# Hybrid attention and DeltaNet decoder trunk on one core: q of the second half in ring tiles, its z projection gated behind the first half's LayerNorm, and a weaker gate for the seven-product MLP

## The chip, the cores and the metric

The kernel runs on one core of one Trainium2 chip. The metric is device time in microseconds (us), the median of the runs of one program. The program before was run three times.

## What is computed

Input x is 1024 tokens by 1024 features in float32; two layers follow each other. Layer 0 is a hybrid mixer, layer 1 a recurrent block, and each is followed by a LayerNorm over `alpha*x + mixer(x)`, a squared-ReLU MLP with 4096 hidden features, and a second LayerNorm over `alpha*x + mlp(x)`.

```python
proj = x @ w_in                                  # layer 0
qa, ka, va, qkv_b, z, beta_logit, a_logit = split_cols(proj, HYB_SPLITS)
o_a = sliding_window_attention(rope(qa), rope(ka), va, sinks)   # 8 query heads, 2 kv heads, window 128
qb, kb, vb = split(silu(causal_dwconv(qkv_b, conv_w)))          # 4 heads of 128
o_b = gated_delta_rule(l2norm(qb), l2norm(kb), vb, g, beta)
o_b = rmsnorm(o_b) * norm_w * silu(z)
mix = concat([o_a, o_b]) @ w_out
...
x = layer_norm(alpha * x + mix)
x = layer_norm(alpha * x + square(relu(x @ w1)) @ w2)
```

## The kernel before

**Halves and streams.** The 1024 tokens are worked as two halves of 512, c = 0 and c = 1. Each half is one Python generator, `stream(c)` (line 1373): hybrid mixer, `mix_out` (output projection and LayerNorm), MLP and LayerNorm of layer 0, then the same for layer 1. Beside the two streams run small generators called mixers: the DeltaNet heads (`head_mid`, line 967), attention (`attn_prep`, `attn_block`), the LayerNorms, and so on. They are spawned by the streams.

**Arithmetic.** Every large product is made of three matmuls on operands that are split into a rounded high part and a rest (`mm3`). A weight block of 128 x 1024 is loaded by SP's DMA queue into a tile `ws` (3 buffers), ScalarE or, for every fifth block, VectorE makes the high part `wh`, VectorE makes the rest `wl` (`wblock`, line 349; 3 buffers each). A projection of 128 features by 512 tokens (`proj_fm`) is 24 matmuls of 512 columns on one weight block. The heads and the attention use plain float32 matmuls and transposes of 32 to 128 columns; in what follows they are the small matmuls. They write to the four `mx` banks, the projections to the four `mm` banks.

**The order on TensorE is a planner's.** `class Clock` (line 60) keeps estimated end times of all operations. The loop at line 1402 takes, at each step, a mixer whose next inputs are ready by that estimate, or else one more product of a stream: of the two streams the one in the earlier phase first, and if that is blocked, the other. TensorE's instructions get a fixed order in this way; VectorE, ScalarE and SP are then put in order by a timeline scheduler. Each engine works its own list strictly in that order on the chip.

**Buffers as gates.** A generator goes on when its buffers are free: `need("g", n)` for n of 14 granules (`g`, 128 x 2048, line 25), and the rings of 128 x 512 tiles `t` (11), `s` (10) and `f` (4, line 29). For c = 0, heads use rings `t` and `s` in turn, for c = 1 only `t`, so of c = 1 one head is in work at a time.

**The order in the hybrid mixer of c = 1** (`hybrid`, line 1269; the branch `if c` follows `zs`). The projections k, q, v of head 0 come first (`head_front`), then k and v of attention (`kv_proj`), then q of attention (`q_proj`, line 760, which puts its four blocks into one granule, `st["qg"]`), then k, q, v of head 1. The projections that cannot be used yet are parked (`park`, line 913): made on TensorE, copied to a tile `r` and stored in DRAM as `parked_b`; six for heads 2 and 3, and four z, one for each head. They are loaded back into `f` tiles when a head wants them: by `head_front` with x = None, and, for the four z, by `zs` (line 1298), which waits until c = 0 has the key `"ln0"`, set in `mix_out` (line 1334) when the granules of the LayerNorm's output are claimed. `head_z` (line 949) works silu(z) out of a loaded block in two ScalarE and two VectorE steps. The rope of `attn_prep` (line 796) reads the q blocks; the granule is given back at the end of `attn_preps` (line 1244).

**The MLP** (`mlp`, line 529) works the 4096 hidden features in four quarters of two parts. `straight(e)` does one part with plain products: four projections of 24 matmuls and 96 matmuls with the second weight. From some even part on, `first(j)` makes the eight hidden projections of a quarter j ahead and `seven(j)` multiplies that quarter in seven instead of eight block products, 168 instead of 192 matmuls, at the price of summed weights made by DMA and of two granules. The loop before stays with `straight` while this does not hold: c = 1 itself, or c = 1 has begun its output projection in this layer, and two granules are free, and the part is even (line 718).

Of the kernel before, what the change touches and what calls it, by code (L numbers as in the profile page):

```python
# [20 lines left out]
CH = 512  # L21
NT = CH // P
KT = D // P
ALPHA = 4 ** 0.25
GB = 14
# [188 lines left out]
def trunk(ctx: ExitStack, tc, I, out):  # L214
# [21 lines left out]
    rings = dict(RINGS, g=GB)  # L236
# [12 lines left out]
    def gran(dt=F32):  # L249
        return take("g", gpool.tile([P, 2048], dt, tag="g", name=nm("g")))  # L250
# [4 lines left out]
    def ts(r, dt=F32):  # L255
        return tl(r, dt)[:, :512]

    def free(r, *tiles):
        rings[r] += len(tiles)
        spare[r] += [t.name for t in tiles]  # L260
        assert rings[r] <= (GB if r == "g" else RINGS[r])

    def need(r, n=1):
        return wait(lambda: rings[r] >= n)
# [4 lines left out]
    def wait(cond):  # L269
        while not cond():  # L270
            yield BLOCK
# [7 lines left out]
    def v4(a):  # L279
        return a.rearrange("p (a b) -> p a b", a=4)  # L280
# [248 lines left out]
    def mlp(layer, c, yT, yg, ls, res, tail=False):  # L529
# [185 lines left out]

        hids = {}
        e = 0
        while e < 8 and not ((c == 1 or sts[1].get("op", -1) >= layer) and rings["g"] >= 2 and e % 2 == 0):
            if e == 7:
                res["start"]()  # L720
            yield from straight(e, e == 7)
            e += 1
# [36 lines left out]

    def q_proj(c, x, st, oT):  # L760
        ps = yield from proj_tm([I["hin_q"][i] for i in range(4)], x, 512)
        st["qg"] = gran()
        for n in range(NT):
            oT.quad(0, n)
            S.copy(st["qg"][:, n * CH:(n + 1) * CH], ps[n])
        yield UNIT

    def kv_proj(c, x, st, oT, pre):
# [25 lines left out]
        V.tensor_tensor(x4[:, :, :, 1, :], a4[:, :, :, 1, :], b4[:, :, :, 0, :], ALU.add)  # L794

    def attn_prep(c, n, st, tl, o):
        q, kr = v4(st["qg"][:, n * CH:(n + 1) * CH]), st["k"][n]
        yield from need("f", 2)
        a, b, qs = tl[n % 2], ts("f"), v4(ts("f"))
        rope(kr.unsqueeze(1), kr.unsqueeze(1), 1, n, a[:, :128], b[:, :128])  # L800
        rope(qs, q, 4, n, a, b)
        yield at(kr, qs)
        ps = mx_ps()
        PE.transpose(ps[:, :P], kr, ident)
        kT = cpool.tile([P, P], F32, tag="kT", name=nm("kT"), bufs=4)
        V.tensor_copy(kT, ps[:, :P])
        ps = mx_ps()
        for g in range(4):
            PE.transpose(ps[:, g * P:(g + 1) * P], qs[:, g, :], ident)
        free("f", b, qs)  # L810
        S.copy(a, ps)
        o["qT"], o["kT"] = a, kT
        yield at(a, kT)
        o["ok"] = True
# [429 lines left out]
    def attn_preps(c, st, o):  # L1244
        yield from wait(lambda: c == 0 or sts[0].get("att") == 4)
        angles["t"] = clk.tile("angles", 1, cpool.tile([P, 256], F32, tag="angles", name=nm("angles")))
        DA.dma_start(angles["t"], I["angles"][c])
        for n in range(NT):
            yield from wait(lambda: st.get("att", 0) >= n - 1)
            yield from attn_prep(c, n, st, slot["tl"], o[n])  # L1250
        free("g", st["qg"])

    def attention(c, st, oT, o):
        for n in range(NT):
# [14 lines left out]
    def hybrid(c, x, oT, st, rs):  # L1269
        d = [dict() for _ in range(4)]  # L1270
        if c == 0:
            slot["tl"] = slots(8)
            yield from kv_proj(c, x, st, oT, lambda k2: load_xT(c, x, k2))
            DS.dma_start(csb, I["consts"])
        else:
            yield from wait(lambda: "x" in st)
            yield from head_front(c, 0, x, d[0], rs[0])
            yield from wait(lambda: sts[0].get("att", 0) >= 2)
            yield from kv_proj(c, x, st, oT, None)
        spawn(delta_scalars(c, st))  # L1280

        def q():
            yield from need("g", 3)
            yield from q_proj(c, x, st, oT)
            o = [dict() for _ in range(NT)]
            spawn(attention(c, st, oT, o))
            spawn(attn_preps(c, st, o))
        def begin(h):
            yield from wait(lambda: h - st.get("scan", 0) < len(rs))
            spawn(head_mid(c, h, st, d[h], oT, rs[h % len(rs)]))  # L1290

        def later(h):
            yield from begin(h)
            for i in range(h + 1, 4):
                yield from head_front(c, i, None, d[i], rs[0])
                yield from begin(i)

        def zs():
            yield from wait(lambda: "ln0" in sts[0])
            yield from need("g", 2)  # L1300
            oT.quad(1, 0)
            for h in range(4):
                yield from head_z(h, None, oT, d[h])

        def mixer(g):
            spawn((r if r is not UNIT else lambda: 0.0) for r in g)

        if c:
            yield from q()
            yield from begin(0)  # L1310
            yield from head_front(c, 1, x, d[1], rs[0])
            mixer(later(1))
            mixer(zs())
            for h in (2, 3):
                for j in range(3):
                    yield from park(h * 4 + j, x)
            for h in range(4):
                yield from park(h * 4 + 3, x)
        for h in range(0 if c else 4):
            yield from head_front(c, h, x, d[h], rs[h % len(rs)])  # L1320
            yield from begin(h)
            if h == 1:
                yield from q()
                yield from need("g", 2)
                yield from head_z(0, x, oT, d[0])
                yield from head_z(1, x, oT, d[1])
                spawn(load_x(1, xTs[1]))
        if c == 0:
            yield from head_z(2, x, oT, d[2])
            yield from head_z(3, x, oT, d[3])  # L1330
        x.free()
        yield from wait(lambda: st.get("mids") == 4 and st.get("att") == 4)

    def mix_out(w, oT, resid, which, r, s, t, hold):
        yield from after(t)
        yield from need("g", 2)
        s["yg"] = [gran() for _ in range(2)]
        ls = ln_stats()
        s["yT"] = ActT()
        f = dict(n=0, start=lambda: spawn(layernorm(s["yg"], ls, which, r, s["yT"], f)))  # L1340
        yield from out_proj(w, oT, resid, s["yg"], ls, f)
        s["ln0"]["op"] = which // 2
        yield from wait(hold)
        yield from need("g", 4)
        s["yT"].claim()
        s["ln0"]["ln0"] = True
        yield from wait(lambda: "done" in f)

    def mlp_ln(layer, c, s, r, last):
        ls = ln_stats()  # L1350
# [22 lines left out]
    def stream(c):  # L1373
        s = dict(ln0=st[c])
        xT, oT = xTs[c], ActT()
        yield from hybrid(c, xT, oT, st[c], ("t", "s") if c == 0 else ("t",))
        yield from mix_out(I["hout"], oT, lambda n: I["x"][c * CH + n * P:c * CH + (n + 1) * P, :], 0,
                           "s" if c == 0 else "t", s, st[c]["t"], lambda: c == 0 or "m7" in sts[0])
        phase[c] = 1
# [168 lines left out]
```

## Time and profile before

| what | value |
|---|---|
| median of 3 runs | 2271.6 us (2271.26 to 2272.66) |
| profiled execution, its own time | 2273.03 us |
| its span on the core | 2271.3 us |
| matmul busy / weight load busy | 97% / 79% of the span |
| VectorE (DVE) / ScalarE (ACT) busy | 68% / 46% |
| mean granted TensorE clock | 0.994 |

The profile is taken in one execution, whose own time is 1.7 us above its span and 1.4 us above the median of the runs. Matmuls overlap and their ends are modelled, so 97% busy is no measure of how dense they are. Engines are PE (matmuls), PEld (weight loads of TensorE), DVE, ACT, POOL and SP. All operations of the rows carry line 178, 206 or 210, the helpers that record them, so they are told apart by their tiles.

### The profile page before, as it was taken

The page shows a single profiled execution, that of the slowest core. Times are in us where ns is not written, and L with a number is a line of the kernel's source. Part 1 is how long each engine was busy: PE and PEld are TensorE (multiplying, and loading weights), DVE is VectorE, ACT ScalarE, POOL GpSimd, SP SyncE. Part 2 cuts the span into 40 slices and gives each one's busy share as a digit, 9 for nine tenths or more (in the row PEclk, how much of TensorE's full clock was granted, in tenths as well). Part 3 has the DMA queues.
Part 4 walks back from the last instruction along what each step waited for, and adds up shares of the span by engine and source line. Part 5 has one row for each costly group of instructions (what it writes and reads, how often), then busy time and mean ns, then how long its engine had stood idle before and what let it go on. Part 6 is the DMA issues. An engine that isn't in the chain of part 4 may idle for free.

```text
span 2271.3 us, 31951 instructions
## 1 busy us (share of the span) xinstructions
PE 2210.8 (97%) x12436; PEld 1787.7 (79%) x12436; DVE 1546.5 (68%) x2809; ACT 1049.1 (46%) x1878; POOL 28.9 (1%) x56
## 2 busy tenths in 40 slices
PE   8999999979999999999999999999999999999997
PEld 7767877757878887888888878778788887888886
DVE  7787776576555567586567898685565657776477
ACT  5465456244422344454444677373434444444442
POOL 0000000000000000000000000000000000000000
PEclk9999999999999999999999999999999999999999
DMA  4121223256677666677775333323523443444341
GB/s 168 59 78 39 94 77 115 81 171 185 192 200 225 207 215 199 208 255 222 232 216 184 130 130 129 122 75 102 181 98 127 140 144 128 150 169 145 122 165 66
DMA packets 89944, 337.46 MB, mean 149 GB/s; under 512 B 9920, under 2 KB 10304, under 8 KB 81600
## 3 DMA queue, kind: packets, MB, share of 16 engines
q1 hardware_dynamic: 76688, 280.56, 35.7%
q0 software_dynamic: 4608, 33.56, 7.8%
q10 hardware_dynamic: 8496, 21.30, 2.7%
q8 instruction: 97, 1.59, 0.3%
q14 instruction: 55, 0.45, 0.1%
HBM read 324.37 MB, written 78.12 MB: 177 GB/s over the span
## 4 chain that ended last, share of the span: by engine, by line
PE 86%; DVE 8%; ACT 4%; DMA 1%; issue 1%; SPq 0%; ACTq 0%; DVEq 0%
PE mm L206 67%; PE mx L206 17%; DVE g L178 2%; PE mx L210 2%; DVE wl L178 1%; DVE s L178 1%; ACT g L178 1%; DVE t L178 1%; DVE f L178 1%; ACT s L178 1%; ACT wh L178 1%; DMA parked<-r 1%; ACT t L178 1%; ACT f L178 0%; DMA f<-parked 0%
## 5 line engine op out<-in xcount | busy, mean ns | idle before, releaser
L206 PE MATMUL mm<-g,wh 128*128 128x512 f32 x2816 | 883.7, 395 | 2.4 <-ACT g L178 1.2
L178 DVE TENSOR_TENSOR wl<-ws,wh 128x1024 fp32r<-128x1024 f32 (+1 forms) x444 | 538.9, 1214 | 395.7 <-ACT wh L178 391.0
L178 ACT CAST wh<-ws 128x1024 fp32r<-128x1024 f32 (+1 forms) x356 | 371.4, 1043 | 685.2 <-PE mm L206 587.0
L206 PEld LDWEIGHTS mm<-g,wh 128*128 128x128 f32 x2816 | 520.3, 188 | 110.0 <-DVE g L178 3.1
L206 PE MATMUL mm<-g,wl 128*128 128x512 f32 x1408 | 549.6, 390 | 0.0
L206 PE MATMUL mm<-wh,s 128*128 128x512 f32 x1152 | 376.9, 394 | 0.7 <-DVE g L178 0.7
L206 PEld LDWEIGHTS mm<-g,wl 128*128 128x128 f32 x1408 | 264.6, 188 | 55.8
L206 PEld LDWEIGHTS mm<-wh,s 128*128 128x128 f32 x1152 | 217.0, 188 | 46.5 <-ACT s L178 1.1
L206 PE MATMUL mm<-wh,g 128*128 128x512 f32 (+1 forms) x768 | 239.7, 383 | 6.4 <-ACT wh L178 6.2
L206 PE MATMUL mm<-wl,s 128*128 128x512 f32 x576 | 225.1, 391 | 0.0
L206 PE MATMUL mx<-wh,s 128*128 128x512 f32 x576 | 188.0, 392 | 1.2 <-DVE s L178 1.2
L206 PEld LDWEIGHTS mm<-wh,g 128*128 128x128 f32 x768 | 142.9, 191 | 33.4 <-ACT wh L178 6.2
L178 ACT CAST s<-g 128x512 fp32r<-128x512 f32 x172 | 104.7, 622 | 105.5 <-PE mm L206 53.5
L178 DVE TENSOR_TENSOR s<-g,s 128x512 fp32r<-128x512 f32 x172 | 116.4, 688 | 45.0 <-ACT s L178 44.9
L206 PE MATMUL mm<-wl,g 128*128 128x512 f32 (+1 forms) x384 | 144.1, 375 | 0.4 <-DVE wl L178 0.4
L206 PEld LDWEIGHTS mx<-wh,s 128*128 128x128 f32 x576 | 108.2, 188 | 24.0 <-DVE s L178 2.0
L206 PEld LDWEIGHTS mm<-wl,s 128*128 128x128 f32 x576 | 108.6, 189 | 21.4 <-issue 0.2
L206 PE MATMUL mx<-wl,s 128*128 128x512 f32 x288 | 112.2, 390 | 0.0
L178 DVE CAST wh<-ws 128x1024 fp32r<-128x1024 f32 x88 | 60.5, 688 | 69.2 <-PE mm L206 62.4
L178 DVE TENSOR_TENSOR g<-g,mm 128x512 f32<-128x512 f32 x136 | 89.4, 684 | 13.4 <-PE mm L206 12.8
L178 ACT ACTIVATE g<-mm 128x512 f32<-128x512 f32 x100 | 59.1, 591 | 77.0 <-PE mm L206 77.0
L206 PEld LDWEIGHTS mm<-wl,g 128*128 128x128 f32 x384 | 73.3, 191 | 11.8 <-DVE wl L178 0.7
(234 smaller groups left out, 2397.3 us busy)
## 6 DMA issues: line engine op xcount, KB each, us to landing
ws<-w SPq DMA_DIRECT2D x232, 512.0 KB, 3.3
ws<-t SPq DMA_DIRECT2D x96, 512.0 KB, 3.4
t<-w POOLq DMA_DIRECT2D x32, 1024.0 KB, 9.0
ws<-hin_fm SPq DMA_DIRECT2D x32, 512.0 KB, 3.3
t<-w SPq DMA_DIRECT2D x16, 1024.0 KB, 7.1
t<-t SPq DMA_DIRECT2D x16, 1024.0 KB, 7.3
ws<-rin SPq DMA_DIRECT2D x32, 512.0 KB, 3.3
ws<-hout SPq DMA_DIRECT2D x16, 512.0 KB, 3.5
```

Source lines behind the costliest of these rows:

```text
L178: r = f(*a, **k)
L206: ins = self.pe.matmul(out, lhsT, rhs, start=start, stop=stop, skip_group_check=fresh)
L210: return self._pe(self.pe.transpose(out, x, ident), out, [x], 0.00042 * 2 * out.shape[-1])
```

## The change

Four things are done. In the half c = 1, `q_proj` writes its four blocks to four tiles of ring `s` (each given back once its rope is done) instead of a granule, and waits for two granules and four `s` tiles instead of three granules; while the `s` tiles are not free, up to six of the parked projections of heads 2 and 3 are made ahead of it. The output projection of c = 0 waits until the projections of head 1 of c = 1 are done (`"front"`). The z of c = 1 wait for the end of the LayerNorm of c = 0 (`"lnd"`) instead of its start (`"ln0"`). And the seven-product form of the MLP may begin, in layer 0, also when three of the four heads of c = 1 are through their scan and four granules are free.

```diff
@@ mlp
-        while e < 8 and not ((c == 1 or sts[1].get("op", -1) >= layer) and rings["g"] >= 2 and e % 2 == 0):
+        room = lambda: rings["g"] >= (2 if c == 1 or sts[1].get("op", -1) >= layer else
+                                      4 if layer == 0 and sts[1].get("scan", 0) >= 3 else GB)
+        while e < 8 and not (room() and e % 2 == 0):
@@ q_proj
-        st["qg"] = gran()
+        if c == 0:
+            g = st["qg"] = gran()
+            st["q"] = [g[:, n * CH:(n + 1) * CH] for n in range(NT)]
+        else:
+            st["q"] = [ts("s") for _ in range(NT)]
         for n in range(NT):
             oT.quad(0, n)
-            S.copy(st["qg"][:, n * CH:(n + 1) * CH], ps[n])
+            S.copy(st["q"][n], ps[n])
@@ attn_prep
-        q, kr = v4(st["qg"][:, n * CH:(n + 1) * CH]), st["k"][n]
+        q, kr = v4(st["q"][n]), st["k"][n]
...
         rope(qs, q, 4, n, a, b)
+        if c:
+            free("s", st["q"][n])
@@ attn_preps
-        free("g", st["qg"])
+        if c == 0:
+            free("g", st["qg"])
@@ hybrid
-            yield from need("g", 3)
+            yield from need("g", 3 - c)
+            yield from need("s", 4 * c)
...
         def zs():
-            yield from wait(lambda: "ln0" in sts[0])
+            yield from wait(lambda: "lnd" in sts[0])
...
         if c:
+            ahead = [h * 4 + j for h in (2, 3) for j in range(3)] + [h * 4 + 3 for h in range(4)]
+            while rings["s"] < 4 and len(ahead) > 4:
+                yield from park(ahead.pop(0), x)
             yield from q()
             yield from begin(0)
             yield from head_front(c, 1, x, d[1], rs[0])
+            st["front"] = True
             mixer(later(1))
             mixer(zs())
-            for h in (2, 3):
-                for j in range(3):
-                    yield from park(h * 4 + j, x)
-            for h in range(4):
-                yield from park(h * 4 + 3, x)
+            for b in ahead:
+                yield from park(b, x)
@@ mix_out
         yield from wait(lambda: "done" in f)
+        s["ln0"]["lnd"] = True
@@ stream
+        if c == 0:
+            yield from wait(lambda: "front" in st[1])
```

No engine has more or fewer instructions than before: 10842 matmuls in the program's list of both, of the same shapes, and 2809 on DVE. Four copies and the sixteen rope products that read them have an `s` tile where they had a granule. Up to the end of `kv_proj` of c = 1, TensorE's list is the same. In the output projection of c = 0 lies the main difference: before, `q_proj`, three projections and six parked ones stand between `kv_proj` and it; now two parked ones, `q_proj`, three projections and one parked one. Behind it stand four parked ones before and seven now.

**SP's list, from the end of q_proj to the first block of the output projection.** `ws` is a weight block, `hin_q` the weight of q, `hin_fm` of the other projections, `hout` of the output projection, `r` the tile that is parked. Before:

```order
L178 DMA ws_447_3315<-hin_q 128x1024
L178 DMA ws_457_3364<-hin_fm 128x1024
L178 DMA ws_490_3539<-hin_fm 128x1024
L178 DMA ws_501_3653<-hin_fm 128x1024
L178 DMA ws_505_3692<-hin_fm 128x1024
L178 DMA ws_512_3764<-hin_fm 128x1024
L178 DMA ws_527_3913<-hin_fm 128x1024
L178 DMA ws_545_4044<-hin_fm 128x1024
L178 DMA ws_553_4093<-hin_fm 128x1024
L178 DMA ws_565_4162<-hin_fm 128x1024
L178 DMA parked_8_3760<-r_511_3761 128x512
L178 DMA ws_591_4301<-hout 128x1024
```

Now, from the second of the two parked ones that stand ahead of q_proj:

```order
L178 DMA ws_435_3215<-hin_fm 128x1024
L178 DMA ws_447_3286<-hin_q 128x1024
L178 DMA ws_451_3325<-hin_q 128x1024
L178 DMA ws_455_3364<-hin_q 128x1024
L178 DMA ws_458_3394<-hin_q 128x1024
L178 DMA parked_8_3211<-r_434_3212 128x512
L178 DMA ws_470_3437<-hin_fm 128x1024
L178 DMA parked_9_3278<-r_442_3279 128x512
L178 DMA ws_505_3647<-hin_fm 128x1024
L178 DMA ws_514_3726<-hin_fm 128x1024
L178 DMA ws_518_3765<-hin_fm 128x1024
L178 DMA ws_531_3829<-hout 128x1024
```

Nine projections stood between q and the output projection, four stand there now.

**DVE's list at the end of the LayerNorm of c = 0.** Splits of its transposed output are the rows `g<-mx` (before g_660 and g_662, now g_632 and g_634); `f` tiles and the rows that read them are z; `wl` with `ws_738` before, and with `ws_698`, `ws_722`, `ws_731` now, is a weight block of the MLP. Before:

```order
L178 TENSOR_TENSOR g_662_4821<-mx_699_5050,g_661_4820 128x4x128
L178 TENSOR_TENSOR g_660_4819<-mx_700_5063,g_659_4818 128x4x128
L178 TENSOR_TENSOR t_612_4413<-mx_701_5082,csb_75 128x128
L178 TENSOR_TENSOR g_668_4833<-f_683_4941,g_667_4832 128x512
L178 TENSOR_TENSOR g_662_4821<-mx_702_5100,g_661_4820 128x4x128
L178 TENSOR_TENSOR wl_740_5390<-ws_738_5387,wh_739_5389 128x1024
L178 TENSOR_TENSOR t_612_4413<-t_612_4413,mx_706_5142 128x128
L178 SCALAR_TENSOR_TENSOR f_693_5030<-f_693_5030,f_694_5031 128x512
L178 STREAM_TRANSPOSE t_612_4413<-t_612_4413 128x128
L178 TENSOR_TENSOR g_668_4833<-f_693_5030,g_667_4832 128x512
L178 TENSOR_TENSOR t_612_4413<-mx_707_5161,csb_75 128x128
L178 TENSOR_TENSOR g_660_4819<-mx_708_5179,g_659_4818 128x4x128
```

Now:

```order
L178 TENSOR_TENSOR g_634_4604<-mx_670_4884,g_633_4603 128x4x128
L178 TENSOR_TENSOR g_632_4602<-mx_671_4894,g_631_4601 128x4x128
L178 TENSOR_TENSOR wl_685_4984<-ws_683_4981,wh_684_4983 128x1024
L178 TENSOR_TENSOR wl_700_5035<-ws_698_5032,wh_699_5034 128x1024
L178 SCALAR_TENSOR_TENSOR f_704_5044<-f_704_5044,f_705_5045 128x512
L178 TENSOR_TENSOR wl_724_5157<-ws_722_5154,wh_723_5156 128x1024
L178 SCALAR_TENSOR_TENSOR f_706_5051<-f_706_5051,f_707_5052 128x512
L178 TENSOR_TENSOR g_703_5043<-f_704_5044,g_702_5042 128x512
L178 TENSOR_TENSOR g_703_5043<-f_706_5051,g_702_5042 128x512
L178 TENSOR_TENSOR t_479_3461<-g_702_5042,g_703_5043 128x512
L178 TENSOR_TENSOR wl_733_5248<-ws_731_5245,wh_732_5247 128x1024
L178 TENSOR_TENSOR g_634_4604<-mx_688_5016,g_633_4603 128x4x128
```

The rows before hold the second to the fifth of the eight splits, with two of the four z among them and the others behind; now no z stands ahead of the seventh split (`mx_671`), and two stand between it and the eighth (`mx_688`).

**SP's list at the start of the output projection of c = 1.** `w1_0` and `w2_0` are the MLP's weights. Before:

```order
L178 DMA ws_997_7180<-w2_0 128x1024
L178 DMA ws_1005_7228<-w2_0 128x1024
L178 DMA ws_1008_7258<-w2_0 128x1024
L178 DMA t2_0_2_115<-t1_0_2_113 128x2048
L178 DMA ws_1018_7304<-hout 128x1024
```

Now:

```order
L178 DMA ws_1010_7254<-w2_0 128x1024
L178 DMA ws_1015_7290<-w1_0 128x1024
L178 DMA t4_0_2_116<-t2_0_2_115 128x2048
L178 DMA ws_1020_7333<-w1_0 128x1024
L178 DMA ws_1031_7377<-hout 128x1024
```

Two of the eight hidden projections of the first seven-product quarter have moved ahead of the output projection of c = 1. The quarter itself is the same one, the third: four parts are straight before it in both.

## Rows read from the trace of the kernel before

**Rows 1.** The page: its span and busy times.

```profile
span 2271.3 us, 31951 instructions
PE 2210.8 (97%) x12436; PEld 1787.7 (79%) x12436; DVE 1546.5 (68%) x2809; ACT 1049.1 (46%) x1878; POOL 28.9 (1%) x56
```

**Rows 2.** Stages by their windows: length, busy us of PE, PEld, DVE, ACT and POOL with the number of instructions, granted clock, DMA share, GB/s. The stages are the projections and parked ones ahead of the output projection of c = 0, the stretch behind it up to the MLP's first matmul, and the four straight parts.

```profile
290.00:380.10 90.10, 87.40 (x745) 62.97 (x744) 62.21 (x172) 44.91 (x123) 0.00 (x0) 1.00 0.30 100
...
443.00:486.70 43.70, 34.61 (x377) 27.80 (x375) 38.01 (x96) 20.57 (x35) 0.00 (x0) 0.88 0.47 164
486.70:711.20 224.50, 220.56 (x1660) 175.87 (x1661) 131.37 (x294) 82.67 (x184) 10.17 (x14) 1.00 0.69 195
```

**Rows 3.** The same columns, in slices of 10 us around the MLP's first matmul, and in a stretch of the seven-product MLP.

```profile
470.00:480.00 10.00, 3.49 (x94) 2.43 (x95) 8.74 (x15) 4.05 (x7) 0.00 (x0) 0.78 0.98 375
480.00:490.00 10.00, 8.49 (x152) 6.30 (x143) 7.16 (x14) 4.84 (x11) 0.00 (x0) 0.71 0.54 166
490.00:500.00 10.00, 7.17 (x58) 5.32 (x56) 8.12 (x15) 3.29 (x7) 1.03 (x2) 1.00 0.29 74
...
1000.00:1250.00 250.00, 249.37 (x1114) 205.66 (x1113) 168.23 (x203) 112.33 (x156) 6.78 (x10) 1.00 0.70 215
```

**Rows 4.** Whom PE waited for from 443 to 500 us: total us, times, longest us.

```profile
PE mx L206 <- DVE t L178: 9.3, 4, 3.9
PE mx L206 <- DVE lnw L178: 1.4, 1, 1.4
PE mm L206 <- ACT g L178: 1.2, 1, 1.2
PE mm L206 <- DVE g L178: 0.3, 1, 0.3
```

**Rows 5.** PE in order of time: start us, us, engine, line, operation, out<-in, shape, count, and in brackets the idle time before it with what ended it. The first two rows are the first matmuls of two parked projections, 24 matmuls apart; 486.73 is the MLP's first matmul; 699.28 is the last row of small matmuls in the four straight parts.

```profile
443.00 0.62 PE L206 MATMUL mm<-g,wh 128*128 128x512 f32 x2
...
448.44 0.62 PE L206 MATMUL mm<-g,wh 128*128 128x512 f32 x2
...
471.01 0.45 PE L206 MATMUL mx<-t 32*32 32x32 f32 x32
471.39 0.66 PE L210 MATMUL mx<-csb,g 128*128 128x128 f32 x4
471.80 0.71 PE L206 MATMUL mm<-g,wh 128*128 128x512 f32 x2
472.35 0.40 PE L206 MATMUL mm<-g,wl 128*128 128x512 f32 x1
475.36 0.51 PE L206 MATMUL mx<-t 32*32 32x32 f32 x32 [2.61 <-DVE t L178]
479.76 0.65 PE L206 MATMUL mx<-t 32*32 32x32 f32 x32 [3.90 <-DVE t L178]
480.34 1.11 PE L210 MATMUL mx<-csb,g 128*128 128x128 f32 x4
...
486.73 0.50 PE L206 MATMUL mm<-g,wh 128*128 128x512 f32 x1 [1.17 <-ACT g L178]
...
699.28 0.60 PE L210 MATMUL mx<-csb,t 128*128 128x128 f32 x4
```

**Rows 6.** DVE in order of time, the same columns. 446.21 is the last statistics operation of the output projection of c = 0, 488.29 the last split of its LayerNorm.

```profile
446.21 0.64 DVE L178 BATCH_NORM_STATS2 lns<-g 128x6 f32<-128x512 f32 x1
...
452.15 0.15 DVE L178 TENSOR_TENSOR lnw<-lnw 128x2 f32<-128x2 f32 x1
452.22 0.15 DVE L178 SCALAR_TENSOR_TENSOR lnw<-lnw 128x2 f32<-128x2 f32 x1
...
470.27 0.69 DVE L178 TENSOR_TENSOR g<-mx,g 128x512 fp32r<-128x512 f32 x1
470.87 1.29 DVE L178 TENSOR_TENSOR g<-g,s 128x512 f32<-128x512 f32 x2
472.07 1.23 DVE L178 TENSOR_TENSOR wl<-ws,wh 128x1024 fp32r<-128x1024 f32 x1
473.21 0.69 DVE L178 TENSOR_TENSOR g<-g,s 128x512 f32<-128x512 f32 x1
...
478.70 0.69 DVE L178 SCALAR_TENSOR_TENSOR f<-f,f 128x512 f32<-128x512 f32 x1 [0.87 <-ACT f L178]
480.08 0.69 DVE L178 TENSOR_TENSOR g<-f,g 128x512 fp32r<-128x512 f32 x1 [0.46 <-ACT g L178]
482.11 0.69 DVE L178 TENSOR_TENSOR g<-mx,g 128x512 fp32r<-128x512 f32 x1 [1.14 <-ACT g L178]
484.85 0.69 DVE L178 SCALAR_TENSOR_TENSOR f<-f,f 128x512 f32<-128x512 f32 x1 [1.51 <-ACT f L178]
...
488.29 0.69 DVE L178 TENSOR_TENSOR g<-mx,g 128x512 fp32r<-128x512 f32 x1
```

**Rows 7.** DVE, two reductions of attention scores in a row, in the half c = 0, where such blocks stand close together.

```profile
215.37 0.42 DVE L178 CUSTOM_DVE_ANT_0 g<-mx,csb 128x256 f32<-128x256 f32 x1
...
215.71 0.42 DVE L178 CUSTOM_DVE_ANT_0 g<-mx,csb 128x256 f32<-128x256 f32 x1
```

**Rows 8.** ACT in the stretch behind the output projection of c = 0: the tanh of a z and what it waited for.

```profile
478.04 0.63 ACT L178 ACTIVATE f<-f 128x512 f32<-128x512 f32 x1 [3.94 <-DMA f<-parked]
```

**Rows 9.** Whom PE waited for from 500 to 711.2 us, the straight parts without their first 13 us; the answer has this one row.

```profile
PE mx L206 <- DVE t L178: 0.7, 1, 0.7
```

## The prediction

> **What bounds the kernel now.** The page first: matmuls are busy 97% of the span, no other engine over 68% [rows 1]. TensorE is the bound, and the change neither adds nor takes away a matmul, so the time can move only by what TensorE waits, in the part whose order changes: from the end of `kv_proj` of c = 1 (263 us) to the output projection of c = 1 (755 us). Next the stages, to see where in it TensorE waits: the nine projections ahead of the output projection of c = 0 are idle 2.7 us of 90.1, the four straight parts 3.9 of 224.5, but the 43.7 us behind that output projection 9.1 us, at a granted clock of 0.88 [rows 2]. In slices, nearly all of it lies between 470 and 500 us [rows 3].
>
> Then the waits and the order in time tell what happens there. The output projection ends at 443.0. Four parked projections follow, and at 472.35 the last of their matmuls starts. The next thing in TensorE's list of any length is the MLP, at 486.73; between lie only small matmuls of a DeltaNet head and the last transposes of the LayerNorm [rows 5]. The MLP wants the normalised, transposed output. So the LayerNorm of c = 0 ends last, and it takes from the last statistics (446.85) to its last split (488.98), 42.1 us on VectorE [rows 6]. VectorE is busy 38.0 of these 43.7 us [rows 2]. In its last quarter VectorE's idle time is 0.87, 0.46, 1.14 and 1.51 us, 4.0 in all, three of them at a row of z and one at a split [rows 6]: ScalarE's tanh of z waits for the parked block to come back from DRAM (3.94 us once) [rows 8], and the splits of the LayerNorm stand behind it in two lists that are worked in order.
>
> **The size of the gap.** From the end of the last parked matmul (472.35 + 0.23) to 486.73 are 14.15 us. The work in it is four groups of 32 small matmuls and 16 transposes. At full clock a group takes 0.38 us and four transposes 0.41 us (471.01 to 471.39 to 471.80) [rows 5], so 4 x 0.38 + 4 x 0.41 = 3.2 us are work and **11.0 us are lost**. Of these, 2.61 + 3.90 + 1.17 = 7.7 us are waits; the rest is mainly the clock: granted 0.78 and 0.71 in the two slices, partly at the 1.2 GHz level [rows 3], where the group at 479.76 takes 0.58 us. The other waits from 443 to 500 us are 12.2 - 7.7 = **4.5 us** [rows 4], one at 459 and the rest in the MLP's first 11 us.
>
> A second measure: in 470 to 500 us PE is idle 30 - 19.2 = 10.9 us [rows 3]. The Trainium skill ("Perfetto Trace Analysis", Identifying the Most-Contended Engine) calls matmul busy time a poor measure and takes the weight loads instead; those are busy 14.1 us here and 0.823 of a dense stretch [rows 3], so 24.7 - 14.1 = 10.6 us would be missing, and a sum by that would take 10.6 where the counted rows give 11.0 and 3.2 for the same 30 us. I take the counted rows, since they price the small matmuls one by one.
>
> **The change, part by part.**
>
> *q in `s` tiles and the early output projection.* The copies and rope products have the same shapes: nothing. Two parked projections stand ahead of q now; they fill TensorE while the `s` tiles of the other half's last head are in use. The output projection of c = 0 comes three parked projections earlier, so three more lie behind it: seven instead of four. A parked projection is 24 matmuls in 5.44 us [rows 5], so 16.3 us of dense work move from a place where TensorE waited little into the gap of 11.0 us. On SP the weight blocks and stores move with them, in the same number.
>
> *Does the LayerNorm stay as long?* VectorE's list holds 91 instructions from the last statistics to the last split before, 117 now. Prices are distances from start to start: 0.60 us for 512 columns, 1.13 for a `wl`, 0.07 (0.16 if it waits for the one before) for a small one, 0.34 for a reduction of scores [rows 6, 7]. Now 33 x 0.60 + 7 x 1.13 + one `wh` 0.60 + 8 x 0.34 + 60 x (0.07 to 0.16) = 35.2 to 40.6 us (a reduction is two instructions): the small ones are many, since a head's norm is woven into that of the LayerNorm. To it comes what VectorE idles: at best nothing, at worst the 4.0 us of now, and 3.9 us from the end of the output projection to the start of the count (446.85 less 443.0). So the eighth split ends 39 to 49 us behind the output projection. TensorE's cover is 7 x 5.44 = 38.1 us, plus 69 small matmuls and transposes at 0.11 us [rows 5], 7.6, plus the first 12 matmuls of the MLP, which don't read the eighth split, 2.7: 48.4 us. The sum is nearly covered at its upper end; I take 1.5 us of waiting left.
>
> *z behind the LayerNorm.* All four z stood among the splits; now two stand ahead of the eighth. They can still hold it: their loads are behind two stores on SP. That is in the 1.5 us.
>
> *The MLP's first 11 us and the wait at 459.* 4.5 us now. The first straight block will again stand beside a head's small steps, z and the last attention block, so I keep half: 2.3 us gained, bounds 0 and 4.5.
>
> *A head of c = 1 later.* Ahead of the MLP's first matmul 144 more small matmuls are still undone; the straight parts carry 614 instead of 470. All in all 1053 stand between `kv_proj` and the second output projection in both, so TensorE's work is the same. Price: no row shows this denser order. The nearest is the same stage with 470, which waited 0.7 us over 211 us [rows 9]; the upper bound is a rival below. I take 1.3 us for it and for the other new places.
>
> *Seven products.* The part that the words promise doesn't come: the first quarter done in seven products is the third one in both lists. Two hidden projections go ahead of the second output projection and leave the place behind it: nothing, and a cover of 10.9 us for the last head, as the two blocks without small matmuls at the end of the straight parts were (from 699.28 on, [rows 5]).
>
> **Sum.** 11.0 - 1.5 + 2.3 - 1.3 = 10.5 us less. The profiled execution took 2273.03 us, 1.7 us above its span, so 2262.5; the median of the runs lies 1.4 us lower, 2271.6, so **2261 us**.
>
> **The rivals.**
>
> *A: VectorE takes half back.* The longer list behind the output projection idles as long as now, and waits for TensorE at eight reductions of scores besides, some 0.5 us each: 3.9 + 40.6 + 4.0 + 4 = 52.5 against a cover of 48.4, so 4 us of waiting, and nothing gained in the MLP's first block: 11.0 - 4.1 - 1.3 = 5.6 us less, 2266 us. For it: VectorE is the fullest engine there [rows 2]. Against it: most of its idle time was z's.
>
> *B: no change.* The seven parked projections stand in front of the MLP, but their own `wl` stand behind the LayerNorm in VectorE's list; that of the sixth is behind 58 small and 24 wide operations. If these run at the upper price, with the idle time, TensorE waits between parked projections for what it waited for before the MLP. It needs 10 us of it: 2270 us. Against it: the same count to that `wl` gives 25 to 30 us, so 29 to 34 behind the output projection, and TensorE gets there after 5 x 5.44 + 65 x 0.11 = 34 us.
>
> *C: slower, the last head becomes the bound.* Heads of c = 1 are worked one at a time. Before, 470 small matmuls went by from 486.7 to 700, 2.2 in a us. If that pace were the chain's own, 614 would take 279 us; TensorE has 768 x 0.227 + 614 x 0.107 + 10.9 = 251 us to put beside them (0.227 is 5.44 / 24, and 0.107 what is left for each of the 470 small ones in 224.5 us [rows 2]). It would wait 28 us in the second output projection's place: 2261 + 28 = 2289 us. The point is a pace of 2.45 in a us; below 2.35 it eats all that is won. Against it: TensorE waited 0.7 us there [rows 9], so the pace was set by TensorE's own list, not by the chain.
>
> **How the numbers follow.** Forecast 0.57, A 0.20, B 0.13, C 0.10. A run of this kernel can tell 0.2%, 4.5 us. The forecast's own range is 2256 (all of 11.0 and 4.5 won) to 2265; A and B carry the range up to 2270, C is left out: 2255 to 2270, the lower end with 1 us for the spread of the runs. Faster by over 0.2% is the forecast and most of A, 0.75; the same is the rest of A and B, 0.15; slower 0.10.
>
> **What would show it.** Right: no gap over 3 us and a granted clock of 1.00 around the MLP's first matmul; it comes 45 to 51 us behind the output projection of c = 0, which starts 16 us or more before 380; waits of PE from the output projection to 13 us into the MLP fall from 12.2 us to about 5; the last z's loads no longer stand among the splits. The MLP's seven-product part looks as before, shifted by about 10 us. Wrong: waits of parked matmuls for `wl` (B), of the MLP's first matmuls for the splits over 3 us (A), or of small matmuls late in the straight parts, over 5 us in sum (C).

## The result and the profile after

The changed kernel takes **2279.8 us** (median of 5 runs, 2277.6 to 2283.2) against 2271.3 us of the kernel before on the same chip: ratio **1.0036**, 95% interval 1.0025 to 1.0048. It is slower by 8.6 us; the forecast was 2261, within 2255 to 2270. The profiled execution took 2282.2 us.

The page hardly shows it: TensorE's share is that of [rows 1], and all engines' instructions are as many.

```profile
span 2280.4 us, 31958 instructions
PE 2215.7 (97%) x12436; PEld 1789.9 (78%) x12436; DVE 1545.0 (68%) x2809; ACT 1048.5 (46%) x1878; POOL 28.6 (1%) x56
```

The stages do. The columns are those of [rows 2]; the stages are: from the end of `kv_proj` to the output projection of c = 0, that projection, the seven parked blocks, the four straight parts, and the second output projection with two hidden blocks. First the kernel after, then the kernel before, which was asked for the same five stages (its third and fourth are in [rows 2]).

```profile
263.90:334.00 70.10, 68.61 (x446) 55.91 (x445) 48.43 (x155) 34.27 (x96) 0.00 (x0) 1.00 0.29 96
334.00:416.00 82.00, 78.09 (x575) 55.59 (x574) 49.86 (x124) 35.90 (x98) 0.00 (x0) 0.96 0.19 62
416.00:475.90 59.90, 54.47 (x261) 41.33 (x259) 41.91 (x128) 31.88 (x76) 0.00 (x0) 0.94 0.33 111
475.90:719.60 243.70, 235.28 (x1931) 183.48 (x1929) 140.93 (x312) 87.42 (x196) 10.18 (x14) 0.99 0.67 189
719.60:774.60 55.00, 55.00 (x246) 45.38 (x245) 24.30 (x36) 11.20 (x13) 3.27 (x4) 1.00 0.87 261
```

```profile
263.40:380.10 116.70, 113.67 (x878) 85.00 (x877) 82.31 (x246) 55.73 (x153) 0.00 (x0) 1.00 0.30 102
380.10:443.00 62.90, 62.90 (x299) 44.69 (x298) 33.71 (x96) 31.78 (x94) 0.00 (x0) 1.00 0.21 72
...
711.20:765.80 54.60, 54.60 (x242) 45.09 (x241) 28.83 (x63) 11.03 (x12) 2.85 (x3) 1.00 0.69 208
```

Over the five stages TensorE does the same work in both: 502.4 us before, 510.7 now, so 8.3 us of the loss lie here. Idle time grew from 16.1 to 19.3 us, and busy time from 486.3 to 491.5: the same matmuls took 5.1 us more. The granted clock is below 1 in three of the five stages now, and was in one before.

The gap ahead of the MLP did go. Its first matmul starts at 475.9 instead of 486.73 and waits for nothing. But three places lose in its stead. TensorE in order of time, columns as in [rows 5]:

```profile
436.13 1.07 PE L206 MATMUL mx<-g,vraw 128*64 128x512 f32 x2 [1.33 <-ACT g L178]
437.13 1.16 PE L206 MATMUL mx<-kT,g 64*128 64x128 f32 x16
442.19 1.94 PE L210 MATMUL mx<-csb,g 128*128 128x128 f32 x8 [3.89 <-DVE g L178]
443.78 1.20 PE L206 MATMUL mm<-g,wh 128*128 128x512 f32 x2
...
450.30 0.62 PE L206 MATMUL mm<-g,wh 128*128 128x512 f32 x2
...
475.88 0.71 PE L206 MATMUL mm<-g,wh 128*128 128x512 f32 x2
...
491.37 1.11 PE L210 MATMUL mx<-csb,t 128*128 128x128 f32 x4 [6.87 <-DVE t L178]
492.14 1.20 PE L206 MATMUL mm<-g,wh 128*128 128x512 f32 x2
```

(`vraw` and `kT` are attention's v and k, `csb` holds the identity for transposes. A float32 product, unless it is a transpose, stands as two records: `x2` at 436 is one product of the program's list, `x16` at 437 are eight.) At 436 an attention product waits for its probabilities, at 442 the LayerNorm's transposes wait for a place to write to, both in the third of the seven parked blocks; at 491 the transposes of a head's v wait 6.87 us, inside the MLP. Behind the last two waits, the pair of matmuls that takes 0.62 us at 450 takes 1.20: the granted clock is partly at its 1.2 GHz level. Slices of 10 us, columns as in [rows 3]; the first two lie in the output projection of c = 0, behind waits of 1.6 and 1.9 us:

```profile
340.00:350.00 10.00, 9.51 (x123) 5.61 (x123) 3.88 (x9) 0.59 (x1) 0.00 (x0) 0.83 0.18 55
360.00:370.00 10.00, 8.39 (x63) 6.33 (x63) 6.71 (x29) 1.62 (x6) 0.00 (x0) 0.83 0.23 79
...
440.00:450.00 10.00, 7.81 (x39) 6.53 (x40) 6.57 (x19) 1.76 (x3) 0.00 (x0) 0.66 0.16 52
...
490.00:500.00 10.00, 8.63 (x30) 6.27 (x31) 8.84 (x17) 5.04 (x11) 0.00 (x0) 0.71 0.10 29
```

Before, the low clock lay in the gap itself [rows 3], where there was little to slow down; now it lies on dense matmuls.

Where do the waits come from? First ScalarE, then VectorE, in order of time:

```profile
430.56 5.05 ACT L178 ACTIVATE g<-g,lnw 128x512 f32<-128x512 f32 x7 [4.29 <-DVE lnw L178]
435.51 0.57 ACT L178 COPY g<-mx 128x512 f32<-128x512 f32 x1
...
480.46 0.63 ACT L178 ACTIVATE f<-f 128x512 f32<-128x512 f32 x1 [2.94 <-DMA f<-parked]
...
489.36 0.63 ACT L178 ACTIVATE f<-f 128x512 f32<-128x512 f32 x1 [6.89 <-DMA f<-parked]
```

```profile
432.65 6.70 DVE L178 TENSOR_TENSOR g<-g,s 128x512 f32<-128x512 f32 x11
439.28 1.22 DVE L178 TENSOR_TENSOR wl<-ws,wh 128x1024 fp32r<-128x1024 f32 x1
...
441.36 0.68 DVE L178 TENSOR_TENSOR g<-mx,g 128x512 fp32r<-128x512 f32 x1
...
477.72 0.68 DVE L178 TENSOR_TENSOR g<-mx,g 128x512 fp32r<-128x512 f32 x1
...
490.02 0.69 DVE L178 SCALAR_TENSOR_TENSOR f<-f,f 128x512 f32<-128x512 f32 x1 [6.83 <-ACT f L178]
490.63 0.68 DVE L178 TENSOR_TENSOR t<-mx,t 128x512 f32<-128x512 f32 x1
```

Attention's copy at 435.51 stands behind seven activations of the LayerNorm.

The transposes at 442 want one of the four `mx` banks. By the program's lists all four are taken there: one by the LayerNorm's first transposes, one by attention's output, two by attention's scores. The first comes free with the split at 441.36, which ends 0.15 us before the transposes start and stands behind eleven norm operations, a `wl`, a twelfth norm operation and a reduction of scores on VectorE.

The 6.87 us are z: the tanh waits 6.89 us for a parked block, z's product on VectorE waits for the tanh, and the head's `t<-mx,t` stands behind it in the same list. That operation empties the `mx` bank that the transposes at 491 write to; the other three hold another product of the head and attention's work. The block is the z that was parked last, and its load cannot go before its own store has landed. SP issues the load at 481.08, and the copy that POOL issued at 480.07 is then under way. The DMA issues from 472 to 500 us (KB of one, median us from issue to landing) say why the block is late:

```profile
t<-w SPq DMA_DIRECT2D x1, 1024.0 KB, 7.0
f<-parked SPq DMA_DIRECT2D x4, 256.0 KB, 7.4
t<-w POOLq DMA_DIRECT2D x1, 1024.0 KB, 9.0
```

`t<-w` are the copies that add up blocks of w2 for the seven products (`w2_sums`, spawned with the MLP). Beside them a load of a parked block takes 7.4 us (median of four).

### The profile page after: what moved, and what is told of

Read it like the earlier page. It is cut to its first block, busy times and chain, and to the rows that moved or that the text cites. A ratio compares the mean times of both kernels' runs of the same rounds, so it can differ in the third digit from the quotient of the medians.

```text
span 2280.4 us, 31958 instructions
## 1 busy us (share of the span) xinstructions
PE 2215.7 (97%) x12436; PEld 1789.9 (78%) x12436; DVE 1545.0 (68%) x2809; ACT 1048.5 (46%) x1878; POOL 28.6 (1%) x56
## 4 chain that ended last, share of the span: by engine, by line
PE 86%; DVE 9%; ACT 3%; issue 1%; DMA 1%; ACTq 0%; DVEq 0%; SPq 0%
PE mm L206 67%; PE mx L206 17%; DVE g L178 3%; PE mx L210 2%; DVE wl L178 2%; DVE s L178 1%; DVE t L178 1%; ACT s L178 1%; DVE f L178 1%; ACT g L178 1%; ACT wh L178 1%; DMA f<-parked 0%; ACT f L178 0%; DVE wh L178 0%; ACT t L178 0%
```

## The experiments

Five theories of the loss were put to runs:

- Theory 1: z, moved into the MLP, holds TensorE up there; 1a: the copies make it late.
- Theory 2: the early output projection loses, since it puts attention and heads beside the LayerNorm.
- Theory 3: the prediction's rival C, a head chain that is too dense.
- Theory 4: the rule on seven products loses.
- Theory 5: q in ring tiles loses.

Ratios are to the kernel before, with 95% intervals; 0.001 is 2.3 us. Each edit is against the changed kernel unless it says otherwise.

**early_no_gate**: the gate undone.

```diff
-            yield from wait(lambda: "lnd" in sts[0])
+            yield from wait(lambda: "ln0" in sts[0])
```

> The changed kernel with only the gate of z undone (z may start when the output of the LayerNorm has its tiles, as before). Theory 1 (z is what the change loses by: behind the gate its round trip through DRAM stands in the in-order lists of the MLP's first blocks, 6.9 us of PE at 491 and a stretch at half clock): 2270 to 2273 us, PE's waits of the first 45 us of the MLP under 2 us. Theory 2 (the early output projection itself loses, by waits and half clock from 334 to 476): 2278 to 2281, the waits before the MLP stay. Theory 3 (the denser head chain beside the straight parts): 2279 to 2282, since the straight parts carry 598 small matmuls here and 614 there.

2275.7 us, **1.0010** (1.0001 to 1.0018). The wait of 6.9 us is gone, and PE waits 2.3 us in the MLP's first 41 us; the waits of 3.9 and 1.3 us stay. The time lies between what theories 1 and 2 said: both have a share.

**gate_no_early**: the kernel before with the gate and the new rule on seven products, nothing else.

```diff
@@ before: zs / mix_out / mlp
-            yield from wait(lambda: "ln0" in sts[0])
+            yield from wait(lambda: "lnd" in sts[0])
...
+        s["ln0"]["lnd"] = True
...
-        while e < 8 and not ((c == 1 or sts[1].get("op", -1) >= layer) and rings["g"] >= 2 and e % 2 == 0):
+        while e < 8 and not (room() and e % 2 == 0):
```

> The kernel before with the gate of z and the rule on seven products, without q in ring tiles, early parked blocks and early output projection: four parked blocks behind the output projection, 594 small matmuls beside the straight parts. Theory 1 (z behind the gate loses in the MLP): 2276 to 2280, a wait of 4 to 8 us in the MLP's first 20 us. Theory 2 (early output projection loses): 2266 to 2270, as the LayerNorm is rid of z. Theory 3 (denser head chain): 2278 to 2282, but the loss spread over the straight parts, with no wait over 3 us at their start.

2264.7 us, **0.9963** (0.9951 to 0.9975): faster than before by 8. Its five stages:

```profile
263.20:379.80 116.60, 113.57 (x877) 84.83 (x877) 82.18 (x245) 55.65 (x153) 0.00 (x0) 1.00 0.30 102
379.80:442.70 62.90, 62.90 (x298) 44.69 (x297) 33.71 (x96) 31.79 (x95) 0.00 (x0) 1.00 0.21 72
442.70:470.40 27.70, 25.96 (x129) 21.18 (x128) 27.34 (x67) 17.41 (x28) 0.00 (x0) 1.00 0.43 143
470.40:702.20 231.80, 229.12 (x1904) 181.59 (x1905) 140.08 (x312) 84.20 (x190) 10.17 (x14) 0.99 0.69 197
702.20:757.20 55.00, 55.00 (x245) 45.39 (x245) 24.26 (x36) 11.18 (x13) 2.45 (x3) 1.00 0.83 261
```

Their sum is 494.0 us instead of 502.4, idle 7.5 instead of 16.1, busy the same. Behind the output projection stand four parked blocks as before, and yet the MLP starts after 27.7 us, not 43.7: VectorE's work there fell from 38.0 [rows 2] to 27.3 us. With z behind the LayerNorm, the head that needs z waits too, and no step of the next head stands among the splits. What is left are short waits at the last splits (whom PE waited for from 442.7 to 500 us):

```profile
PE mm L206 <- DVE g L178: 2.2, 1, 2.2
PE mm L206 <- ACT g L178: 1.3, 1, 1.3
PE mx L210 <- DVE g L178: 0.4, 1, 0.4
```

Theory 3 falls here: 594 small matmuls stand beside its straight parts, and behind 500 us PE waits 0.3 us in them. So the gate, with the rule, is worth 8 us alone and costs 5.9 beside the early projection (1.0036 less 1.0010). The rule without the gate was not run.

**early_z_held**: z's tanh put 8 us behind its load in the planner's order.

```diff
             DS.dma_start(ps, parked[b])
+            t = clk.now + 8.0
+            yield lambda: t
```

> The changed kernel; the only edit is that z's tanh is put into the lists 8 us (by the planner's clock) after its load is issued, so that other work stands in front of it on ScalarE and VectorE while the block comes back from DRAM. Theory 1: the 6.9 us wait at the MLP's start and the half clock behind it go, 2270 to 2274. Theories 2 and 3: 2278 to 2282, whatever becomes of that wait.

2281.6 us, 1.0042 (1.0029 to 1.0054): no gain. The loads are slow still (5.5 us), and another thing now stands behind z in VectorE's list, a copy of attention. From 472.6 to 520 us:

```profile
PE mx L206 <- DVE g L178: 4.7, 1, 4.7
PE mx L206 <- DVE t L178: 3.0, 2, 2.6
PE mx L206 <- ACT g L178: 0.3, 1, 0.3
```

The edit missed theory 1's number and left the cause standing: the block came back no earlier.

**early_no_seven_rule**: the old rule for the seven products (`while` as in the kernel before).

> The changed kernel with the old rule for when seven products may begin. In the order of the instructions the third quarter is then done in straight blocks too: 24 matmuls of 128x512 more, 24 x 0.227 = 5.4 us. If the rule does no more than keep the third quarter in seven products: 2283 to 2287. If the two hidden blocks it puts beside the last head, ahead of the second output projection, are what loses the time (theory 4): 2276 to 2281, the saved loss paying for the 24 matmuls.

2282.7 us, 1.0038 (1.0026 to 1.0050), for 24 matmuls (5.4 us) more. That lies between the two ranges and is inconclusive on theory 4: the other blocks changed ScalarE's and SP's order at the MLP's start as well, and in its profile the wait for z is 0.7 us (parked blocks came back in 4.5). The run shows that the rule keeps one quarter in seven products. It also shows that the wait hangs on the order in those lists, since TensorE's own list is the change's up to the end of the second output projection.

**early_sums_later**: the copies for the sums begin 40 us later.

```diff
     def w2_sums():
...
+        t30 = clk.now + 40.0
+        yield lambda: t30
         for layer, j in ((i, j) for i in range(2) for j in range(4)):
```

> The changed kernel; the only edit is that the 1 MB copies for the sums of w2 begin 40 us (by the planner's clock) later, so that none is in flight while z is loaded. TensorE's order has the same blocks. Theory 1a (the 6.9 us wait in the MLP is a load of z that takes 7.4 us beside those copies, where others take about 3.5): the wait falls to under 3 us and the half clock behind it goes, 2272 to 2276 us. Theory 1b (it is the store and load of z itself, whatever else moves): 2278 to 2281 and the wait stays.

2275.6 us, **1.0014** (1.0005 to 1.0023): theory 1a's number. TensorE's list is the change's throughout; on VectorE and ScalarE some operations changed places from the MLP's start on. So 5.0 us come back. The DMA issues from 472 to 500 us have no copies now, and parked blocks land in half the time:

```profile
f<-parked SPq DMA_DIRECT2D x5, 256.0 KB, 3.5
```

PE's waits from 475.4 to 520 us:

```profile
PE mx L206 <- DVE t L178: 1.9, 1, 1.9
PE mx L210 <- DVE t L178: 0.4, 1, 0.4
```

The Trainium skill ("DMA: Bandwidth & Descriptors", Issuing engines are not separate DMA queues) says that DMAs of SP, ScalarE and GpSimd run on the same 16 engines and interleave, whoever issues them. The trace agrees: beside copies issued by SP and by POOL, SP's small load takes 7.4 us instead of 3.5.

**gate_sums_later** is, in spite of its label, the kernel of gate_no_early once more, as its expectation says.

> The kernel of gate_no_early once more, for one look: its third and fourth load of z are issued ahead of the copies for the sums of w2, so every theory expects 2262 to 2267 us and no wait for z over 2 us in the first 30 us of the MLP.

2264.7 us in one execution, with the same waits of TensorE (2.5, 1.3 and 1.1 us in the longest rows of both).

**early_three_blocks_later**: the output projection waits for three parked blocks more; gate, ring tiles and rule stay.

```diff
-            yield from wait(lambda: "front" in st[1])
+            yield from wait(lambda: "front" in st[1] and len(parked) >= 6)
```

> The changed kernel, but the output projection of c = 0 also waits until six blocks are parked, three later than in the change: four are left behind it, as before, with q in ring tiles, the gate and the rule on seven products kept. Theory 2 (where the output projection stands is what loses, since attention and a head's steps then stand among the LayerNorm's): 2265 to 2271, under 7 us lost from the output projection's end to the MLP. Theory 5 (q in ring tiles, and the two blocks ahead of it, are what loses): 2276 to 2281.

2265.7 us, **0.9969** (0.9958 to 0.9980): theory 2's number, 15.2 us for three blocks (1.0036 less 0.9969); theory 5 falls. Its second and third stage, the output projection and the four blocks behind it:

```profile
369.20:438.20 69.00, 68.83 (x358) 49.64 (x357) 43.63 (x124) 37.64 (x112) 0.00 (x0) 1.00 0.22 69
438.20:470.70 32.50, 32.37 (x153) 23.07 (x152) 30.21 (x74) 20.84 (x37) 0.00 (x0) 1.00 0.37 118
```

TensorE idles 0.2 and 0.1 us there, at a clock of 1.00; the change idles 3.9 and 5.4 us in the same two stages, at 0.96 and 0.94.

**early_attention_behind_ln**: attention of c = 1 starts no tile during the LayerNorm.

```diff
         for n in range(NT):
+            yield from wait(lambda: c == 0 or "op" not in sts[0] or "lnd" in sts[0])
             yield from attn_block(c, n, st, oT, slot["tl"], o[n])
```

> The changed kernel, but attention of c = 1 starts no new tile while the LayerNorm of c = 0 runs; the last tile of it goes into the MLP's first block. Theory 2 in its narrow form (attention's steps among the LayerNorm's make its 3.9 and 1.3 us waits and its half clock): 2272 to 2277, waits between the output projection and the MLP under 2 us. If the same waits only move into the MLP with the tile: 2278 to 2283.

2274.8 us, **1.0012** (1.0003 to 1.0021): 5.4 us back, the number of theory 2's narrow form. The wait for the transposes falls from 3.89 to 0.70 us; the one of the tile already begun stays, and one of 2.0 us comes in the MLP's first part, where the last tile now stands:

```profile
436.60 1.07 PE L206 MATMUL mx<-g,vraw 128*64 128x512 f32 x2 [1.33 <-ACT g L178]
...
442.23 0.66 PE L210 MATMUL mx<-csb,g 128*128 128x128 f32 x4 [0.70 <-DVE g L178]
```

**early_sums_and_attention**: both edits.

> The changed kernel with both edits at once: the copies for the sums of w2 begin 40 us later, and attention of c = 1 starts no tile while the LayerNorm of c = 0 runs. Alone they gave back 5.0 and 5.4 us of the 8.2. If the two losses are separate: 1.0036 - 0.0022 - 0.0024 = 0.999, 2268 to 2272 us. If both are one loss (the wait that ends last is the same): no better than either alone, 2274 to 2277. What is then still above 0.9963 is the price of the output projection's own place.

2270.5 us, 0.9992 (0.9982 to 1.0002), inside the range for separate losses: together the edits give back 10.0 us, a little more than the 8.6 that the change lost. The traces don't bear that separation out. With attention held alone, the wait behind z has gone too (0.2 us): that edit also puts the last parked block behind the first projection of the MLP. And the five stages take 509.8 us with it and 510.6 with both edits (the last stage has two hidden blocks more there). So the 5.4 us are not the price of attention beside the LayerNorm alone, and where the second edit's further 4.5 us lie stays open.

**Three more with the copies 40 us later**: the output projection behind six and behind five parked blocks, and gate_no_early.

> The kernel of early_three_blocks_later (output projection behind six parked blocks, four left behind it) with the copies for the sums of w2 40 us later. Its waits for z in the MLP were already short, so theory 1a expects little: 2262 to 2266 us; if copies cost the MLP's first blocks in general (weights too), 2256 to 2261.

> The same with the output projection behind five parked blocks instead of six, so five are left behind it, and 20 of the last tiles' attention steps stand beside the LayerNorm. Theory 2 (attention and heads beside the output projection and the LayerNorm lose): between the changed kernel without the copies (1.0014) and the one above, 2264 to 2271 us. If one block more of cover is worth more than it loses: 2257 to 2262.

> The kernel of gate_no_early with the copies for the sums of w2 40 us later: its loads of z stand ahead of the copies already, so theory 1a expects no change, 2263 to 2267 us. If copies cost the MLP's first blocks in general: 2258 to 2262.

Behind six blocks 2264.2 us, **0.9962** (0.9949 to 0.9974); behind five 2269.4, 0.9983 (0.9974 to 0.9991); the change, behind three, 1.0014 (early_sums_later). Of these three places, each earlier one costs more. gate_alone_sums_later missed: 2268.6, 0.9985 (0.9976 to 0.9994), though up to 795 us its trace is that of gate_no_early. What the later copies cost behind that isn't settled.

**heads_held_z_as_before**: the kernel before with the new rule; head 1 waits for the LayerNorm, z does not.

```diff
@@ before: later
         def later(h):
+            yield from wait(lambda: "lnd" in sts[0])
             yield from begin(h)
```

> The kernel before with the rule on seven products and one edit: head 1 of c = 1 and those after it begin only when the LayerNorm of c = 0 is done, while z stays where it was, among the LayerNorm's splits. The gate held back both, and made 8.0 us. If it was z's round trip (VectorE's idle rows at z, 4.0 us, and the waits they make): 2270 to 2273 us, the MLP's first matmul still 38 us or more behind the output projection. If it was the heads' steps, which are off VectorE's list then (VectorE is busy 27.3 us instead of 38.0 in that stretch): 2262 to 2266, the first matmul 28 to 32 us behind it. Between, 2266 to 2270: both.

2273.0 us, 1.0003 (0.9994 to 1.0012). The stretch behind the output projection:

```profile
442.90:474.70 31.80, 27.42 (x135) 22.38 (x133) 31.44 (x74) 19.03 (x32) 0.00 (x0) 0.94 0.49 157
```

31.8 us instead of 43.7, VectorE busy 31.4 instead of 38.0: in this stretch the heads are the larger part of what the gate takes away (6.6 us of VectorE's 10.7) and z the rest. But the time is not won: the heads come later, seven hidden blocks, none before, stand ahead of the second output projection, and TensorE waits 1.6 us for a `wl` further on. So neither theory's whole line came, and how the 8 us of the gate divide between z and heads stays open.

## Why the prediction was wrong

**The gap: right, but not by cover.** The MLP's first matmul waits no more, 59.9 us behind the output projection (forecast 45 to 51). The forecast laid three more parked blocks, 16.3 us, into a gap of 11.0. gate_no_early shows that the gap closes without them. "Does the LayerNorm stay as long?" counted the changed kernel's list, 117 instructions with a head's norm among them, as given. It did not ask what the gate alone would leave of that list. With the gate alone the stretch is 27.7 us; four blocks nearly fill it, and the three others cover nothing. In the change the price of the list held (VectorE is busy 41.9 of the 59.9 us), but its idle time did not: 18.0 us instead of at most 7.9 (3.9 ahead of the count and 4.0 in it). The eighth split, at 477.72, ended 62.4 us behind the output projection, not 39 to 49, and yet nothing waited for it.

**The parked blocks as cover: mis-sized.** If the 38.1 us for seven blocks are right, the 7.6 for 69 small matmuls and transposes, 0.11 each, were not. TensorE is busy 54.47 us in that stage, so they took 16.4, some 0.24 each, a part of it at the lower clock. An attention product of 512 columns takes 1.07 us (two records) and eight score products 1.16 (sixteen records, rows above); the price came from 32x32 steps and transposes. On top come 5.4 us of waits where 1.5 were left.

**The early output projection: costed at nothing. This is the step that failed.** "*q in `s` tiles and the early output projection*" priced its three blocks as work that moves into the gap, at no cost elsewhere. It did not ask what those blocks had kept apart: attention and the head of c = 1, which ran beside parked blocks before, now run beside the output projection and the LayerNorm. The output projection takes 82.0 us instead of 62.9; most of that is work moved there, 3.5 us are waits, and two slices are at clock 0.83. Given the gate, the early place costs 15.2 us by early_three_blocks_later, and 16.6 by gate_no_early (1.0036 less 0.9963). Holding attention gives 5.4 us back and moving the copies 5.0, together 10.0; how the rest divides is not shown.

**z "in the 1.5": wrong.** The text kept z among the LayerNorm's last splits and named the stores ahead of its loads. Two z now come back inside the MLP's first blocks, where the copies begin. The last one's load does stand behind its store, but it then takes twice as long as without copies; the wait is 6.87 us plus the low clock behind it. The sign named for rival A, waits over 3 us of the MLP's first matmuls for the splits, didn't show; the long wait is that of a head's transposes, for an `mx` bank.

**The MLP's first 11 us: 2.3 us of gain didn't come**, for that reason. **Denser heads: 1.3 us were enough.** The straight parts carry 144 small matmuls more by the program's list, PE waits 0.3 us in them behind 520 us, and rival C, the only one that was slower, is not what happened. **Seven products:** the same quarter in both, as said; but the rule is what keeps it there once the order shifts (early_no_seven_rule).

B's waits of parked matmuls didn't come either (0.2 us, for a `wh`). None of the rivals asked what the moved blocks had kept apart, so none held the case that came.

## What to carry to other kernels

Before laying more work over a late chain, look at what stands in that chain's in-order lists by chance: taking it off (0.9963) closed the gap that three more blocks of cover closed only at a loss. A block that is moved leaves a place as well: price what now stands together, at the operations' own durations, and what the low clock does to the dense work behind each new wait. Count the banks too: two of the three waits in the rows above were for an `mx` bank that other work held. When a small load on a chain moves, ask which large transfers start at its new place.

The best versions run, 0.9963 (gate_no_early) and 0.9962 (output projection behind six blocks, copies later), lie some 8 us below the kernel before and 16 below the change, and cannot be told apart.

## What the hardware showed unexpectedly

A 256 KB load from DRAM lands in 3.5 us where no copy runs and in 7.4 us beside two copies of 1 MB from DRAM to DRAM (7.0 and 9.0 us). Behind several waits of 1.6 to 7 us the granted clock was low for a while, a second loss, but not in every execution. In the same order of instructions on TensorE, the output projection of c = 0 took 82.0 us at 0.96 and, in the profile of early_z_held, 79.2 at 1.00:

```profile
333.80:413.00 79.20, 75.36 (x576) 53.94 (x575) 50.03 (x125) 35.93 (x99) 0.00 (x0) 1.00 0.20 66
```
